# Decay factors of two SSD groups made during the gate products, scans done in place

## The chip, the cores and the metric

The kernel runs on one core of one Trainium2 chip. The metric is the device time of one execution in microseconds (us). The kernel before was timed three times: 1971.74, 1972.97 and 1973.63 us, median 1972.97. One further execution was profiled.

The core has five engines that each follow a queue of instructions in order: TensorE (PE), VectorE (DVE), ScalarE (ACT), GpSimd (POOL) and SyncE (SP, which here only issues transfers). ScalarE and GpSimd issue transfers too, in their place in the queue: a transfer that has to wait for something holds up what stands behind it on its engine.

## The reference

One layer of an encoder on 512 positions of 2048 channels, in float32. Beside an attention branch it has a state space branch (SSD) that runs over the sequence forwards and backwards, 32 heads in 4 groups, in 4 chunks of 128 positions:

```
da   = dt * a                                   # per head and position
a_cs = cumsum(da) within a chunk
lmat = exp(segsum(da))                          # lmat[l, s] = exp(a_cs[l] - a_cs[s]) for s <= l, else 0
y_diag = einsum("bclgn,bcsgn->bcgls", C, B) * lmat  applied to x * dt
y_off  = C . state at the chunk's start . exp(a_cs)
y      = y_fwd + y_bwd + d_skip * x ;  y = rmsnorm(y * silu(z))      # z, g_ssm, g_attn = h @ w_in columns
out    = x + (sigmoid(g_ssm) * (y @ w_ps) + sigmoid(g_attn) * (attn @ w_pa)) @ w_o ;  final rmsnorm
```

The decay factors are the point here: for each head and chunk a 128 x 128 matrix of exponentials of running sums of da, forwards below the diagonal and backwards above it, which multiplies the matrix C.B of that chunk.

## The kernel before, in words

Every matrix product is made of three matmuls on halves: a float32 operand is split into a high part (ScalarE casts it, `wh`, `s_h`, `xw_h`) and a low part (VectorE subtracts it, `wl`, `s_l`, `xw_l`). Weights come in tiles of 128 x 1024; three tiles each of `wh` and `wl` go round (L161-162, L535-536). The stages, in us of the profiled execution:

- up to about 113: the norm, the transposes, then the columns x, B and C of group 0 and dt. `dt_make` (L302-327) makes da for all heads and writes it to the scratch `da_d` in DRAM.
- 113 to 557, **the gates**: three products (z, g_ssm, g_attn: `wz`, `wgs`, `wga`), each as seven Strassen products P1 to P7 for each of two column pairs, 42 products of four chunks of 12 matmuls. A chunk's weights are loaded (X, Y or wraw), added where Strassen wants a sum, cast and subtracted (`wh` L458, `wl` L459). Results go through SiLU or sigmoid (L834) and are stored (`put`, L288) by ScalarE's queue.
- 560 to 1100, **the SSD groups** 0 to 3 (`ssd_group`). Each has a start (B, C and x loaded and transposed), a *state part* (`state_in` makes xw, `state` adds `loc` into the running states S0 and S1 and splits them into s_h and s_l, `offdiag` multiplies them into `off`), and a *decay part* of eight jobs (`da_load`, `seg_make`, `diag`): a job takes 4 heads of one chunk. Between all of these, `gap()` puts matmuls of other products (the next group's x, B and C; q, k and v; the attention's gate) as fill.
- then attention, and the output products to the end.

A job of the decay part: SP loads two broadcast tiles `da0` and `da1` (128 x 512, every partition the same row); VectorE scans each into a `sum` tile, with a mask `scn` that restarts the sum at the diagonal (L1135), adds the two, the second reversed (L1138), ScalarE takes Exp (L1139), and the result E multiplies G, which is made from C.B and dt (L1144-1146). `diag` has TensorE apply G to x (`yb`), and VectorE adds `yo` into `y` (L1159).

The order of TensorE's instructions is that of the program, written by hand. The other engines' order is made by a scheduler, which places each instruction where its own cost model finds it ready, within the priorities that `high_priority` gives and the order that `keep_in_program_order` fixes. Tiles come from pools with a fixed number of buffers for each tag; a tile's next user waits for the last reader. The `st` pool has tiles that serve one after another as x, B, C columns under way (`xbc`), as the angles `ta` and `tb` of the rotary part, as `dt64` and as `z`.

Of the kernel before, what the change touches and what calls it, by code (L numbers as in the profile page):

```python
# [72 lines left out]
def build(tc, a):  # L73
# [40 lines left out]
    xbc_d = [[scratch(f"xbc_d{g}_{i}") for i in range(6)] for g in range(GROUPS)]  # L114
    qkv_d = [scratch(f"qkv_d{i}") for i in range(10)]
# [175 lines left out]
    da_d = dr.tile([64, SEQ], F32, name="da_d")  # L291
# [8 lines left out]
    def dt_make(new):  # L300
# [21 lines left out]
        for i in range(2):  # L322
            r0, cs = 64 * i, slice(i * HS, (i + 1) * HS)
            act.dma_start(da_d[0:NH, cs], da2[r0:r0 + NH])
            act.dma_start(da_d[NH:64, cs], pl[r0 + NH:r0 + 64])
            act.dma_start(dt_d[0:64, cs], dt2[r0:r0 + 64])
            act.dma_start(dt_d[64:128, cs], da2[r0:r0 + 64])

# [258 lines left out]

    def product(name, op, chunk, extra=None, pre=None):

        used.append((used[-1] + 1) % 4)  # L590
        bs = [b(name) for b in SETS[used[-1]]]
        for m in range(4):
            raw = chunk(m)
            h, l = w_split(raw)
            if extra:
                extra(m, raw)
            if pre and m == 2:
                pre()
            for i in range(2):
                for jj in range(2):  # L600
# [4 lines left out]
                    pe.matmul(bs[i], xh, wl, start=False, stop=False)  # L605
                    pe.matmul(bs[i], xl, wh, start=False, stop=(j == 7))  # L606
                    yield 3
        product_done()
        return bs
# [217 lines left out]
    for tag, n, w in (("X", 4, 1024), ("p1", 2, SEQ), ("p5", 2, SEQ), ("u", 2, SEQ), ("pad", 2, SEQ), ("Y", 4, 1024)):  # L827
        for _ in range(n):
            wx.tile([P, w], F32, tag=tag, bufs=n, name=f"{tag}_place")
# [59 lines left out]
    gates[1].hooks = {(0, "P5"): [angles]}  # L889
# [6 lines left out]
    run(xbc_gen(0, 3, None))  # L896
    for p_ in gates:
        for cp in range(2):
            run(p_.pair(cp))
# [7 lines left out]
    scan_f, scan_b = scn[:, :SEQ], scn[:, SEQ:]  # L907
# [9 lines left out]
    sw = open_pool("sw", reuse_waits="tile")  # L917

# [76 lines left out]
    def ssd_group(g):  # L995
# [122 lines left out]
        das = deque()  # L1118

        def da_load(c, q):  # L1120
            h0 = g * HPG + q * 4
            das.append([])
            for dd in range(2):
                da = sw.tile([P, 4, P], F32, tag=f"da{dd}", bufs=2, name=f"da{dd}")
                src = da_d[dd * NH + h0:dd * NH + h0 + 4, c * P:(c + 1) * P]
                tc.keep_in_program_order(nc.sync.dma_start(da, src.unsqueeze(0).broadcast_to([P, 4, P])))
                das[-1].append(da)

        def seg_make(c, q):

            h0 = g * HPG + q * 4
            sums = []
            for da, mask in zip(das.popleft(), (scan_f, scan_b)):
                sums.append(tmp2("sum"))
                dve.tensor_tensor_scan(sums[-1], flat(da), mask, 0.0, ALU.add, ALU.mult)  # L1135
            sf, sb = (t.rearrange("p (h l) -> p h l", h=4) for t in sums)
            E = sw.tile([P, 4, P], F32, tag="E", bufs=2, name="E")
            dve.tensor_add(E, sf, sb[:, :, ::-1])  # L1138
            act.activation(flat(E), flat(E), AF.Exp)  # L1139
# [25 lines left out]
        da_load(0, 0)  # L1165
        for c in range(TT):
            cb_make(c)
            for q in range(2):
                G = seg_make(c, q)
                if (c, q) != (TT - 1, 1):  # L1170
                    da_load(c + q, 1 - q)
# [683 lines left out]
```

## Time and profile before

| | us |
|---|---|
| median of three runs | 1972.97 |
| the profiled execution | 1969.35 |
| its span, from the first to the last instruction | 1967.6 |
| PE busy in the span | 1925.9 |
| DVE busy | 1465.5 |
| ACT busy | 1031.3 |
| POOL busy | 249.3 |

The clock granted to TensorE was 0.999 of full speed. An engine's row in a timeline gives the start, the duration, the line, the operation, what it writes and reads, and in brackets for how long the engine sat idle before it and what ended that. Rows of consecutive matmuls overlap: each lasts 0.39 us, and the next begins 0.23 us after it. In the waits of an engine, a row gives who waited for which instruction, the total in us, how many times, and the longest.

### The profile page before, as it was taken

To read this page: it belongs to the slowest core of one execution; us is meant where nothing else is said; L and a number is where in the kernel's file an instruction comes from. 1 tells how busy PE (TensorE), PEld (TensorE's weight loads), DVE (VectorE), ACT (ScalarE), POOL (GpSimd) and SP (SyncE) were. 2 spreads that over 40 slices of the span, in tenths; PEclk is the share of its full clock that TensorE was granted. 3 is DMA by queue.
4 is the path that set the end of the run, shared out by engine and by line. 5 is a ranking of instruction groups with operands and counts; after the bars stand their busy time and mean duration, and the time that the engine had idled before them with its cause. 6 is when DMAs were issued, how large, how long until landed. Compare 5 with 4: busy or idle time off the path is not lost.

```text
span 1967.6 us, 24492 instructions
## 1 busy us (share of the span) xinstructions
PE 1925.9 (98%) x8834; PEld 1589.7 (81%) x8834; DVE 1465.5 (74%) x2064; ACT 1031.3 (52%) x1531; POOL 249.3 (13%) x317
## 2 busy tenths in 40 slices
PE   7999999999999999999999999999999999999998
PEld 5888888888878888877888888888877777888886
DVE  7886676776759869789786467676776888879467
ACT  6444445444464856757747444444455455444344
POOL 0011001001112030030210211111021111100011
PEclk9999999999999999999999999999999999999999
DMA  6469669668654644665554857887389787847447
GB/s 217 166 203 256 164 166 246 157 179 246 143 174 146 206 123 158 211 196 184 165 166 138 241 173 200 212 221 203 102 221 317 231 274 278 288 160 241 159 90 169
DMA packets 170233, 383.27 MB, mean 195 GB/s; under 512 B 16704, under 2 KB 66944, under 8 KB 169920
## 3 DMA queue, kind: packets, MB, share of 16 engines
q1 hardware_dynamic: 103680, 234.02, 35.7%
q0 software_dynamic: 30912, 103.82, 23.6%
q10 hardware_dynamic: 35520, 43.87, 6.3%
q8 instruction: 69, 1.13, 0.2%
q14 instruction: 52, 0.43, 0.1%
HBM read 329.55 MB, written 98.17 MB: 217 GB/s over the span
## 4 chain that ended last, share of the span: by engine, by line
PE 81%; DVE 9%; DMA 5%; issue 3%; ACT 2%; POOL 0%; SPq 0%; ACTq 0%; DVEq 0%; POOLq 0%
PE P L605 11%; PE P L606 11%; PE P L604 11%; PE xbc L168 4%; PE xbc L169 4%; PE xbc L170 4%; PE za L170 2%; PE za L168 2%; PE za L169 2%; DVE sum L1135 2%; PE qkv L168 2%; PE qkv L170 1%; PE f L1613 1%; PE qkv L169 1%; PE f L1614 1%
## 5 line engine op out<-in xcount | busy, mean ns | idle before, releaser
L458 ACT CAST wh<-X 128x1024 fp32r<-128x1024 f32 x164 | 172.4, 1054 | 199.4 <-PE P L606 158.6
L459 DVE TENSOR_TENSOR wl<-X,wh 128x1024 fp32r<-128x1024 f32 x164 | 199.7, 1222 | 86.4 <-ACT wh L458 85.9
L164 DVE TENSOR_TENSOR wl<-wraw,wh 128x1024 fp32r<-128x1024 f32 (+2 forms) x150 | 175.0, 1168 | 91.4 <-ACT wh L163 85.8
L163 ACT CAST wh<-wraw 128x1024 fp32r<-128x1024 f32 (+2 forms) x150 | 144.8, 967 | 123.0 <-PE xbc L169 34.4
L459 DVE TENSOR_TENSOR wl<-Y,wh 128x1024 fp32r<-128x1024 f32 x88 | 107.5, 1223 | 66.9 <-ACT wh L458 66.7
L458 ACT CAST wh<-Y 128x1024 fp32r<-128x1024 f32 x88 | 92.6, 1054 | 116.1 <-PE P L606 105.7
L168 PE MATMUL xbc<-h_h,wh 128*128 128x512 f32 x384 | 152.7, 398 | 0.0
L170 PE MATMUL xbc<-h_h,wl 128*128 128x512 f32 x384 | 149.8, 390 | 0.0
L169 PE MATMUL xbc<-h_l,wh 128*128 128x512 f32 x384 | 149.6, 390 | 0.0
L604 PE MATMUL P<-wh,h_h 128*128 128x512 f32 x384 | 149.4, 389 | 0.0
L605 PE MATMUL P<-wl,h_h 128*128 128x512 f32 x384 | 149.4, 389 | 0.0
L606 PE MATMUL P<-wh,h_l 128*128 128x512 f32 x384 | 149.4, 389 | 0.0
L458 ACT CAST wh<-wraw 128x1024 fp32r<-128x1024 f32 x68 | 71.7, 1054 | 111.0 <-PE P L606 58.4
L459 DVE TENSOR_TENSOR wl<-wraw,wh 128x1024 fp32r<-128x1024 f32 x68 | 83.0, 1221 | 59.9 <-ACT wh L458 59.9
L605 PE MATMUL P<-wl,S 128*128 128x512 f32 x288 | 112.2, 389 | 1.1 <-DVE wl L459 1.1
L604 PE MATMUL P<-wh,S 128*128 128x512 f32 x288 | 112.0, 389 | 0.0
L606 PE MATMUL P<-wh,S 128*128 128x512 f32 x288 | 112.0, 389 | 0.0
L170 PE MATMUL za<-h_h,wl 128*128 128x512 f32 x256 | 100.2, 391 | 1.8 <-DVE wl L164 1.8
L168 PE MATMUL za<-h_h,wh 128*128 128x512 f32 x256 | 101.5, 397 | 0.0
L169 PE MATMUL za<-h_l,wh 128*128 128x512 f32 x256 | 99.7, 390 | 0.0
L170 PEld LDWEIGHTS xbc<-h_h,wl 128*128 128x128 f32 x384 | 72.1, 188 | 15.5
L1365 ACT ACTIVATE pr<-s,nm 128x512 f32<-128x512 f32 x64 | 44.1, 689 | 76.7 <-DVE nm L1363 76.6
(746 smaller groups left out, 5079.5 us busy)
## 6 DMA issues: line engine op xcount, KB each, us to landing
wraw<-wi SPq DMA_DIRECT2D x102, 512.0 KB, 3.6
T_wps<-wps POOLq DMA_DIRECT2D x32, 512.0 KB, 11.1
da<-da_d SPq DMA_DIRECT2D x64, 256.0 KB, 4.1
T_wpa<-wpa POOLq DMA_DIRECT2D x32, 512.0 KB, 9.4
wraw<-wps SPq DMA_DIRECT2D x24, 512.0 KB, 6.1
wraw<-wo SPq DMA_DIRECT2D x20, 512.0 KB, 3.3
xbc_d<-xbc ACTq DMA_DIRECT2D x24, 256.0 KB, 2.7
wraw<-wun SPq DMA_DIRECT2D x16, 384.0 KB, 5.4
```

Of the source, the lines that this page charges most:

```text
L163: act.copy(h, raw)
L164: dve.tensor_sub(l, raw, h.bitcast(F32))
L168: pe.matmul(out, wh, xh, start=start, stop=False)
L169: pe.matmul(out, wh, xl, start=False, stop=False)
L170: pe.matmul(out, wl, xh, start=False, stop=stop)
L458: i = act.copy(hi_, raw)
L459: dve.tensor_sub(lo_, raw, hi_.bitcast(F32))
L604: pe.matmul(bs[i], xh, wh, start=(j == 0), stop=False)
L605: pe.matmul(bs[i], xh, wl, start=False, stop=False)
L606: pe.matmul(bs[i], xl, wh, start=False, stop=(j == 7))
L1135: dve.tensor_tensor_scan(sums[-1], flat(da), mask, 0.0, ALU.add, ALU.mult)
L1365: act.activation(pr, s, AF.Exp, bias=nm, scale=SCALE, accum_out=sm_)
```

## The change

It has four parts.

1. The decay factors of groups 2 and 3 (16 jobs) are made while the gate products run, and written to new scratch tensors `e_d`. A list of ticks runs one step of a job ahead of a weight chunk: `e_scan(n, 0)`, `e_scan(n, 1)` (with the add), `e_exp(n)` (Exp, the store, the next load). Three tiles e0, e1 and e2 of the `st` pool are used; all transfers are on ScalarE's queue. The mask `scn` is loaded once more, before the gates. `angles()`, the positions' sines and cosines, is called ahead of the gates rather than from a hook within.
2. `da_d` now has the layout [direction, chunk, head, position], so that a job's source is one row of 2 KB for 4 heads.
3. In the SSD groups 0 and 1, the scans work in place on the loaded tiles (`E`, four buffers), and the add writes into the first. In groups 2 and 3 a job loads one finished tile from `e_d`, and there is no scan, no add and no Exp.
4. In the pool of the SSD groups (`sw`), the places for the tags r, E, G, cbf, cbb, yz, yo and xT are taken first, so that the loaded B, C and x tiles lie at other addresses, over the operand sums of the gates.

The core of the diff:

```diff
-    da_d = dr.tile([64, SEQ], F32, name="da_d")
+    da_d = dr.tile([2, TT, NH, P], F32, name="da_d")
...
-            act.dma_start(da_d[0:NH, cs], da2[r0:r0 + NH])
-            act.dma_start(da_d[NH:64, cs], pl[r0 + NH:r0 + 64])
+            for dd, t in enumerate((da2, pl)):
+                act.dma_start(da_d[dd, 2 * i:2 * i + 2].rearrange("c h l -> h c l"), chunked(t)[r0 + dd * NH:r0 + dd * NH + NH])
...
+    def seg_load(queue, ts, dd, g, c, q):
+        src = da_d[dd, c, g * HPG + q * 4:g * HPG + q * 4 + 4].rearrange("h l -> (h l)")
+        tc.keep_in_program_order(queue.dma_start(ts[dd], src.unsqueeze(0).broadcast_to([P, SEQ])))
+
+    def seg_scan(t, dd):
+        return dve.tensor_tensor_scan(t, t, scn[:, dd * SEQ:(dd + 1) * SEQ], 0.0, ALU.add, ALU.mult)
+
+    def seg_add(f, b):
+        return dve.tensor_add(heads4(f), heads4(f), heads4(b)[:, :, ::-1])
...
         for m in range(4):
+            f = ticks.popleft() if ticks else None
+            if f:
+                f()
             raw = chunk(m)
...
-    gates[1].hooks = {(0, "P5"): [angles]}
...
+    angles()
+    scn = wx.tile([P, 2 * SEQ], F32, tag="scn", bufs=1, name="scn")
+    act.dma_start(scn, a["scn"])
+    e_t = [st(f"e{i}") for i in range(3)]
...
+    def e_room(n):
+        return e_t[n % 2], e_t[2]
+
+    def e_load(n, dd):
+        if n < len(e_jobs):
+            seg_load(act, e_room(n), dd, *e_jobs[n])
+
+    def e_scan(n, dd):
+        pin(seg_scan(e_room(n)[dd], dd))
+        if dd:
+            pin(seg_add(*e_room(n)))
+        else:
+            e_load(n + 1, 0)
+
+    def e_exp(n):
+        t = e_room(n)[0]
+        pin(act.activation(t, t, AF.Exp))
+        pin(act.dma_start(e_d[e_jobs[n]], t))
+        e_load(n + 1, 1)
...
+    free = [i for i in range(4, 156) if i // 4 % 7 not in (1, 3)]
+    for n in range(len(e_jobs)):
+        i = n * (len(free) - 3) // (len(e_jobs) - 1)
+        for k, f in enumerate((lambda n=n: e_scan(n, 0), lambda n=n: e_scan(n, 1), lambda n=n: e_exp(n))):
+            ticks[free[i + k]] = f
...
+    for tag, n, shape in (("r", 6, [P, SEQ]), ("E", 4, [P, SEQ]), ("G", 2, [P, 4, P]), ("cbf", 2, [P, P]), ("cbb", 2, [P, P]),
+                          ("yz", 2, [P, SEQ]), ("yo", 1, [P, TT, SEQ]), ("xT", 1, [P, TT, SEQ])):
...
+        def e_fetch(c, q):
+            if (g, c, q) in e_d:
+                es.append([e_tile()])
+                tc.keep_in_program_order(nc.sync.dma_start(es[-1][0], e_d[g, c, q]))
+            else:
+                es.append([e_tile(), e_tile()])
+                for dd in range(2):
+                    seg_load(nc.sync, es[-1], dd, g, c, q)
...
-                dve.tensor_tensor_scan(sums[-1], flat(da), mask, 0.0, ALU.add, ALU.mult)
...
+            if len(ts) == 2:
+                for dd, t in enumerate(ts):
+                    seg_scan(t, dd)
+                seg_add(*ts)
+                act.activation(ts[0], ts[0], AF.Exp)
```

TensorE's and POOL's orders are unchanged. Elsewhere the scheduler moves instructions. In the listings below a row is a line of the kernel, an operation, and its tiles with their numbers; lines of the changed kernel are shifted (L458 has become L472, L1079 L1136, L1135 L338).

ScalarE at the start of the gates, before. X_945 and X_947 are the weights of the first two chunks of the second product (X0' and X1' below), xbc_d0_3 is the store of group 0's last x columns:

```order
L458 CAST wh_1074<-X_951 128x1024
L860 DMA tb_2284<-pos 32x128
L416 ACTIVATE xbc_1014<-xbc_1014 128x512
L288 DMA xbc_d0_3_96<-xbc_1014 128x512
L458 CAST wh_1101<-X_945 128x1024
L458 CAST wh_1120<-X_947 128x1024
```

and in the changed kernel:

```order
L879 DMA tb_1037<-pos 32x128 x4
L472 CAST wh_1135<-X_966 128x1024
L430 ACTIVATE xbc_1029<-xbc_1029 128x512
L289 DMA xbc_d0_3_96<-xbc_1029 128x512
L472 CAST wh_1162<-X_960 128x1024
L335 DMA e0_1077<-da_d_509 128x512
L472 CAST wh_1181<-X_962 128x1024
```

The four loads of the positions have moved ahead of the cast before, and e0's load has come in between the casts of X0' and X1'; e0 takes the place in the `st` pool that xbc_1029 had, and waits for the store from it.

VectorE in group 0's state part, from the second round's decay of S1 to the third round's s_l, before (left out where the dots are: the second round's xw_l, tmp and wl):

```order
L1075 TENSOR_TENSOR S0_4581<-S0_4581,loc_4682 128x512
L164 TENSOR_TENSOR wl_4820<-wraw_4817,wh_4819 128x1024
L1079 TENSOR_TENSOR s_l_4689<-S0_4581,s_h_4688 128x512
L1075 TENSOR_TENSOR S1_4591<-S1_4591,loc_4692 128x512
L1074 TENSOR_TENSOR S0_4581<-S0_4581,dec_4371 128x512
L1079 TENSOR_TENSOR s_l_4699<-S1_4591,s_h_4698 128x512
...
L1079 TENSOR_TENSOR s_l_4792<-S0_4581,s_h_4791 128x512
L1079 TENSOR_TENSOR s_l_4802<-S1_4591,s_h_4801 128x512
```

and in the changed kernel:

```order
L338 SCALAR_TENSOR_TENSOR E_5031<-E_5031,scn_4495 128x512
L1132 TENSOR_TENSOR S0_4733<-S0_4733,loc_4834 128x512
L1132 TENSOR_TENSOR S1_4743<-S1_4743,loc_4844 128x512
L165 TENSOR_TENSOR wl_4972<-wraw_4969,wh_4971 128x1024
L1136 TENSOR_TENSOR s_l_4841<-S0_4733,s_h_4840 128x512
L338 SCALAR_TENSOR_TENSOR E_5032<-E_5032,scn_4495 128x512
L1136 TENSOR_TENSOR s_l_4851<-S1_4743,s_h_4850 128x512
...
L1136 TENSOR_TENSOR s_l_4944<-S0_4733,s_h_4943 128x512
L338 SCALAR_TENSOR_TENSOR E_5055<-E_5055,scn_4495 128x512
L338 SCALAR_TENSOR_TENSOR E_5056<-E_5056,scn_4495 128x512
L338 SCALAR_TENSOR_TENSOR E_5106<-E_5106,scn_4495 128x512
L1136 TENSOR_TENSOR s_l_4954<-S1_4743,s_h_4953 128x512
```

Five scans of group 0's first jobs, and one add where the dots are, now stand ahead of rows of the state part; the decay of S0 stands behind the second s_l.

VectorE in group 1's state part, before:

```order
L1071 COPY S0_5753<-loc_5749 128x512
L1071 COPY S1_5763<-loc_5759 128x512
L1079 TENSOR_TENSOR s_l_5756<-S0_5753,s_h_5755 128x512
L1074 TENSOR_TENSOR S0_5753<-S0_5753,dec_4371 128x512
L1079 TENSOR_TENSOR s_l_5766<-S1_5763,s_h_5765 128x512
```

and in the changed kernel:

```order
L338 SCALAR_TENSOR_TENSOR E_6186<-E_6186,scn_4495 128x512
L338 SCALAR_TENSOR_TENSOR E_6187<-E_6187,scn_4495 128x512
L338 SCALAR_TENSOR_TENSOR E_6210<-E_6210,scn_4495 128x512
L1136 TENSOR_TENSOR s_l_5884<-S0_5881,s_h_5883 128x512
L341 TENSOR_TENSOR E_6186<-E_6186,E_6187 128x512
L1136 TENSOR_TENSOR s_l_5894<-S1_5891,s_h_5893 128x512
```

Three scans and an add of the decay part have moved in between the copies of the first states and their low halves.

More of the change, by code (lines that the diff above doesn't have):

```diff
@@ L114, in build @@
     xbc_d = [[scratch(f"xbc_d{g}_{i}") for i in range(6)] for g in range(GROUPS)]
+    e_d = {(g, c, q): scratch(f"e_d{g}{c}{q}") for g in range(2, GROUPS) for c in range(TT) for q in range(2)}
     qkv_d = [scratch(f"qkv_d{i}") for i in range(10)]
@@ L826, in build @@
     cols = part_ = wx
-    for tag, n, w in (("X", 4, 1024), ("p1", 2, SEQ), ("p5", 2, SEQ), ("u", 2, SEQ), ("pad", 2, SEQ), ("Y", 4, 1024)):
+    for tag, n, w in (("X", 4, 1024), ("p1", 2, SEQ), ("p5", 2, SEQ), ("u", 2, SEQ), ("scn", 1, 1024), ("Y", 4, 1024)):
         for _ in range(n):
@@ L896, in build @@
     run(xbc_gen(0, 3, None))
+    angles()
+    scn = wx.tile([P, 2 * SEQ], F32, tag="scn", bufs=1, name="scn")
+    act.dma_start(scn, a["scn"])
+    e_t = [st(f"e{i}") for i in range(3)]
+    e_jobs = list(e_d)
+    pin = tc.keep_in_program_order
+    def e_room(n):
[15 more added lines that the diff above has]
+    for dd in range(2):
+        e_load(0, dd)
+    ticks.extend([None] * 168)
+    free = [i for i in range(4, 156) if i // 4 % 7 not in (1, 3)]
[3 more added lines that the diff above has]
+            ticks[free[i + k]] = f
     for p_ in gates:
@@ L917, in build @@
     sw = open_pool("sw", reuse_waits="tile")
+    for tag, n, shape in (("r", 6, [P, SEQ]), ("E", 4, [P, SEQ]), ("G", 2, [P, 4, P]), ("cbf", 2, [P, P]), ("cbb", 2, [P, P]),
+                          ("yz", 2, [P, SEQ]), ("yo", 1, [P, TT, SEQ]), ("xT", 1, [P, TT, SEQ])):
+        for _ in range(n):
+            sw.tile(shape, F32R if tag == "r" else F32, tag=tag, bufs=n, name=f"{tag}_place")
     def tmp2(name, n=SEQ):
@@ L1116, in cb_make, with e_tile @@
             cbs[c] = (cbf, cbb)
[L1118 to L1127, printed above, removed]
+        es = deque()
+        def e_tile():
+            return sw.tile([P, SEQ], F32, tag="E", bufs=4, name="E")
+        def e_fetch(c, q):
[4 more added lines that the diff above has]
+                es.append([e_tile(), e_tile()])
+                for dd in range(2):
+                    seg_load(nc.sync, es[-1], dd, g, c, q)
         def seg_make(c, q):
             h0 = g * HPG + q * 4
[L1132 to L1139, printed above, removed]
+            ts = es.popleft()
+            if len(ts) == 2:
[3 more added lines that the diff above has]
+                act.activation(ts[0], ts[0], AF.Exp)
+            E = heads4(ts[0])
             G = sw.tile([P, 4, P], F32, tag="G", bufs=2, name="G")
@@ L1164, in ssd_group @@
         last = None
-        da_load(0, 0)
+        e_fetch(0, 0)
         for c in range(TT):
```

6 lines of the change are left out of this document (4 added, 2 removed).

## The prediction

> **What bounds the kernel now.** I read the page first, then the busy time by stage, then what TensorE waited for, stage by stage. The page:
>
> ```profile
> span 1967.6 us, 24492 instructions
> ...
> PE 1925.9 (98%) x8834; PEld 1589.7 (81%) x8834; DVE 1465.5 (74%) x2064; ACT 1031.3 (52%) x1531; POOL 249.3 (13%) x317
> ```
>
> TensorE is busy 98% of the span and its program order is the same before and after. So the time can only move by TensorE's waits: each one that goes shortens the kernel by its length, each new one lengthens it. Work taken off VectorE is worth nothing in itself. By stage (stretch in us, its length, busy time of PE, PEld, DVE, ACT, POOL, then clock, DMA share, GB/s):
>
> ```profile
> 113.00:557.00 444.00, 442.86 (x1954) 366.47 (x1953) 310.91 (x319) 212.96 (x239) 53.68 (x66) 1.00 0.71 191
> 557.00:617.00 60.00, 57.91 (x271) 47.46 (x270) 40.28 (x54) 32.38 (x50) 16.38 (x12) 1.00 0.46 155
> 617.00:684.00 67.00, 67.00 (x332) 56.51 (x331) 61.54 (x117) 48.01 (x86) 2.97 (x2) 1.00 0.59 185
> 684.00:740.00 56.00, 54.97 (x259) 45.00 (x258) 37.69 (x52) 33.57 (x60) 15.66 (x11) 1.00 0.45 139
> ```
>
> The gates (first row) leave TensorE 1.1 us of wait in 444. Group 0's decay part (third row) has VectorE busy 61.5 of 67.0 us, and yet TensorE misses nothing. So groups 0 and 1 have no wait there that could be won. Groups 2 and 3 have; these are TensorE's waits from 890 to 950 us, and from 1000 to 1060 us (total, times, longest):
>
> ```profile
> PE yb L1156 <- DVE G L1146: 1.8, 2, 1.1
> PE za L170 <- DVE wl L164: 1.0, 1, 1.0
> PE qkv L170 <- DVE wl L164: 0.3, 1, 0.3
> ```
>
> ```profile
> PE yb L1156 <- DVE y L1159: 1.7, 1, 1.7
> ```
>
> All four have VectorE late, among the scans. That is what part 3 of the change can win: 1.8 + 1.0 + 0.3 + 1.7 = 4.8 us, and no more.
>
> **The change part by part.** The pieces of a job, as VectorE and ScalarE run them (count, then min/median/max in ns):
>
> ```profile
> L1135 DVE TENSOR_TENSOR_SCAN sum<-da,scn x64: 1187/1212/2247, 617.0 to 1032.0; 128x512 f32<-128x512 f32 x64
> L1138 DVE TENSOR_TENSOR E<-sum x32: 660/683/693, 625.2 to 1052.3; 128x512 f32<-128x512 f32 x32
> ```
>
> ```profile
> L1139 ACT ACTIVATE E<-E x32: 613/632/636, 627.3 to 1059.3; 128x512 f32<-128x512 f32 x32
> L1139 ACT ACT_TABLE_LOAD  x21: 1283/1283/1283, 626.0 to 1058.0; - x21
> ```
>
> Groups 2 and 3 lose 32 scans and 16 adds: 32 x 1.21 + 16 x 0.68 = 49.7 us of VectorE, some 25 us per decay part of 60. The waits there are at most 1.7 us each, so I take them all as gone: **-4.8 us**. The bounds are 0 (the new loads arrive late) and -4.8.
>
> *Start of the gates: +2.0 us.* The job's first load, e0, stands on ScalarE's queue between the casts of X0' and X1' (first listing in the section on the change), and it reuses the tile whose last reader is the store xbc_d0_3. ScalarE there, and that store's landing time:
>
> ```profile
> 108.56 0.35 ACTq L288 DMA_DIRECT2D xbc_d<-xbc  x1
> 110.04 1.05 ACT L458 CAST wh<-X 128x1024 fp32r<-128x1024 f32 x1 [1.51 <-DMA X<-wz]
> 113.64 1.05 ACT L458 CAST wh<-X 128x1024 fp32r<-128x1024 f32 x1 [2.55 <-DMA X<-wz]
> ```
>
> ```profile
> xbc_d<-xbc ACTq DMA_DIRECT2D x1, 256.0 KB, 9.1
> ```
>
> The store lands at 108.56 + 9.1 = 117.66. ScalarE then issues the load (0.35) and casts X1' (1.05): 119.06. VectorE's low half (1.22) is ready at 120.3. In the old kernel that half ran at 116.83, and TensorE read it at 118.57:
>
> ```profile
> 116.83 1.22 DVE L459 TENSOR_TENSOR wl<-X,wh 128x1024 fp32r<-128x1024 f32 x1
> ```
>
> ```profile
> 118.57 0.39 PE L605 MATMUL P<-wl,S 128*128 128x512 f32 x1
> ```
>
> ```profile
> 98.00:118.00 20.00, 18.86 (x84) 15.28 (x83) 12.48 (x17) 9.49 (x12) 4.66 (x6) 1.00 1.04 313
> ```
>
> That is a wait of 1.7 us. Further casts queued behind the load are X2' and X3', needed 2.72 us apart, so they follow in its shadow. Two things can shift it: the masks' 512 KB and e0's 256 KB come into a stretch that the DMA engines fill already (share 1.04, 313 GB/s), where 768 KB are 2.5 us; and TensorE's 1.1 us wait just before (in which VectorE waits for the positions) may go, since the positions are now asked for together. Bounds 0 to +4.2 (1.7 + 2.5); I take 2.0, close to the 1.7.
>
> *The gates' body: +1.5 us.* Cadence and margin, from ScalarE, then VectorE, then the landing of the gates' stores:
>
> ```profile
> 183.82 1.05 ACT L458 CAST wh<-X 128x1024 fp32r<-128x1024 f32 x1 [0.61 <-PE P L606]
> 186.54 1.05 ACT L458 CAST wh<-X 128x1024 fp32r<-128x1024 f32 x1 [1.67 <-PE P L606]
> ```
>
> ```profile
> 184.91 1.23 DVE L459 TENSOR_TENSOR wl<-X,wh 128x1024 fp32r<-128x1024 f32 x1 [1.50 <-ACT wh L458]
> ```
>
> ```profile
> DMA to landing us min/median/max: 3.6/4.7/9.6
> ```
>
> A chunk takes 186.54 - 183.82 = 2.72 us. Three tiles each of wh and wl exist, so a cast starts as TensorE lets go of the chunk three back and is needed two chunks later: 2 x 2.72 = 5.44 us, of which cast and subtraction take 2.3. The margin is 3.1 us. A job puts two scans and an add (3.1 us) on VectorE over two or three chunks with 1.5 us idle in each; Exp and two table loads (3.2 us) on ScalarE beside 1.67 idle per chunk. Both fit the margin. What may not fit: in five of the sixteen jobs, the reload of a tile stands on ScalarE's queue one cast behind the store from that tile. Counted from the cast ahead of the store (0), the store goes out at 1.05, lands at 5.75 with the median 4.7, and the reload goes out at 6.1, where the next cast was due at 5.44; in two of the five a table load and a SiLU (1.28 + 0.62) stand ahead of that cast, which is then late by 2.6: just inside 3.1. With the longest landing, 9.6, it is late by 7.5 and TensorE waits 4.4. Five of these would be 22 us, none is 0; one landing in three or four that is too slow by about a microsecond gives the 1.5 that I take. The jobs' added traffic (16 x 768 KB) raises the share of 0.71 and pushes that way.
>
> [...]
>
> *Group 0's state part: +4.8 us.* The scans of groups 0 and 1 are now in place, bound no longer to the sum tiles, and the order brings them ahead of the rows that make s_l (second listing above). Before, VectorE made s_l just in time. Two rows of VectorE, then TensorE's two readers:
>
> ```profile
> 603.86 0.69 DVE L1079 TENSOR_TENSOR s_l<-S,s_h 128x512 fp32r<-128x512 f32 x1
> ...
> 613.66 0.69 DVE L1079 TENSOR_TENSOR s_l<-S,s_h 128x512 fp32r<-128x512 f32 x1 [0.58 <-ACT s_h L1078]
> ```
>
> ```profile
> 604.66 0.44 PE L169 MATMUL off<-s_l,c_h 128*128 128x512 f32 x1
> ...
> 615.63 0.39 PE L169 MATMUL off<-s_l,c_h 128*128 128x512 f32 x1
> ```
>
> Second round: two scans stand ahead (2.42) and the decay of S0 moves behind (0.60), so s_l ends at 604.55 + 1.82 = 606.37, 1.7 late. Third round: from one s_l's end to the next it was 614.35 - 604.55 = 9.80. Added: three scans 3.63, the add 0.60, S0's decay 0.60; its wait of 0.58 for ScalarE goes. So 606.37 + 14.05 = 620.42 against 615.63 + 1.7 = 617.33: 3.1 late. Together 4.8. Bounds: 0, if what TensorE reads is late anyway for another reason, and about +10, if each of the five scans takes the longest row (2.25).
>
> [...] The old trace has no scan in a state part, and I stay with the median.
>
> *Group 1's state part: +1.7 us.* The same order, three scans between the copies and s_l (third listing). VectorE's rows, then TensorE's readers:
>
> ```profile
> 714.77 1.27 DVE L1071 COPY S<-loc 128x512 f32<-128x512 f32 x2
> ```
>
> ```profile
> 720.95 0.39 PE L169 MATMUL off<-s_l,c_h 128*128 128x512 f32 x1
> ...
> 732.53 0.39 PE L169 MATMUL off<-s_l,c_h 128*128 128x512 f32 x1
> ```
>
> First round: 716.04 + 3.63 + two rows of 0.60 and one of 0.68 = 721.55, 0.6 late. The 18 rows up to the second round's s_l are 12.7 us at their old steps, so 734.3 against 732.53: 1.7 in all, the third round then just fits. Bounds 0 and +5.
>
> *The rest: 0.* The loads of da move no engine's work but SP's queue; group 0's first tiles, laid elsewhere, still come behind a weight load that waits for a tile of VectorE, as before; dt64's later load has 100 us of gates to hide in, and would cost its landing, some 5 us as for the gates' stores, without.
>
> Sum: -4.8 + 2.0 + 1.5 + 4.8 + 1.7 = +5.2 us. The profiled execution took 1969.35 us around its span of 1967.6; the sum makes 1974.6 of it, and of the median 1972.97, 3.6 above, **1978.2 us**.
>
> **The rivals.** *The early scans cost nothing* (0.30). In the stages with the state parts VectorE idles 60.0 - 40.28 = 19.7 us and 56.0 - 37.69 = 18.3: if the rows it waits for there (s_h, loc) are what really sets s_l, the scans fall into the idle time. Then -4.8 remains, plus up to 3.5 from the gates: 1968.2 to 1971.7, the middle 1969. This is the faster side. Against it: the s_l of 603.86 shows no wait ahead of it.
>
> *The reloads' stores land at the long end* (0.08): the five reloads hold ScalarE, 4 to 22 us more: 1990.
>
> *The decay parts keep their waits* (0.08): the change takes the scans away, and the loads from e_d, one per job on SP's queue behind weights, arrive late instead. 1978.2 + 4.8 = 1983.
>
> [...]
>
> **How the numbers follow.** The forecast has 0.50, with its own range from 1973 to 1985. A measurement of this kernel tells 0.2% (3.9 us) from no change. Of the forecast's half, 0.33 is slower by more than that and 0.17 within; of the first rival, 0.24 faster and 0.06 within; the other three (0.20) are slower. So faster 0.24, same 0.23, slower 0.53. The range goes from the full gain without loss, 1967.5, up to the middle of the long rivals, 1988.
>
> **What would show it.** Right: in the new trace TensorE waits for wl near 119 us, for s_l (L1136) in groups 0 and 1 by some 6 us, and has no G, y or wl wait left in groups 2 and 3. Wrong: s_l is in time with scans ahead of it; or TensorE waits for wl or wh all along the gates; or waits for G remain after 890 us, now behind SP's loads of E.

## The result, and the profile after

The changed kernel takes 2002.44 us (median of four runs, 1998.89 to 2005.67), against 1973.28 for the kernel before on the same chip: ratio 1.015, 95% interval 1.0137 to 1.0164. The prediction had 1978.2, with a range up to 1988: the sign is right, the size is not. The profiled execution took 2005.67 us. One execution of kernel K below took 3115.45 us at a granted clock of 0.656 and is left out of its ratio. From the page of the changed kernel, span and engines:

```profile
span 2003.9 us, 24562 instructions
...
PE 1943.4 (97%) x8834; PEld 1595.0 (80%) x8834; DVE 1465.7 (73%) x2064; ACT 1050.2 (52%) x1545; POOL 248.8 (12%) x317
```

The span grew by 36.3 us, and TensorE, with the same 8834 matmuls, is busy 17.5 us longer. So the loss has two parts: 18.8 us in which TensorE waits, and 17.5 us more of busy time for the same work. The same stages as in the prediction, moved to where they lie now (stretch in us, its length, busy time of PE, PEld, DVE, ACT, POOL, then clock, DMA share, GB/s):

```profile
113.00:585.00 472.00, 455.23 (x1955) 369.37 (x1955) 353.94 (x367) 254.83 (x282) 53.57 (x66) 0.99 0.75 207
585.00:652.00 67.00, 60.14 (x271) 47.85 (x270) 47.42 (x60) 37.02 (x54) 16.90 (x13) 0.99 0.42 142
...
719.00:782.00 63.00, 58.91 (x262) 46.55 (x261) 48.00 (x64) 36.88 (x65) 17.36 (x11) 0.97 0.43 138
```

The gates went from 444 to 472 us. TensorE's idle time in them from 1.1 to 16.8 (472.00 - 455.23), and its busy time from 442.9 to 455.2: 15.7 us of waits and 12.4 us of added busy time. Group 0's state part went from 60 to 67 us (waits from 2.1 to 6.9), group 1's from 56 to 63 (1.0 to 4.1). What TensorE waited for, in the gates, then in the two state parts (total, times, longest):

```profile
PE P L624 <- DVE wl L473: 12.3, 14, 2.1
PE P L623 <- ACT wh L472: 4.4, 3, 2.5
...
PE off L170 <- DVE s_l L1136: 3.8, 4, 2.1
...
PE off L170 <- DVE s_l L1136: 1.9, 4, 0.7
PE off L169 <- ACT s_h L1135: 1.3, 2, 0.7
```

From 922 to 1100 us, groups 2 and 3, TensorE has no wait for G, y or wl any more. Behind the gates' waits stand ScalarE and VectorE, both waiting for transfers of the jobs (100 to 610 us; first ScalarE's waits, then VectorE's):

```profile
ACT L853 <- DMA e_d<-e: 12.2, 2, 6.7
ACT wh L472 <- DMA e<-da_d: 12.0, 2, 6.5
...
ACT wh L472 <- DMA xbc_d<-xbc: 6.3, 1, 6.3
ACT wh L472 <- DMA e_d<-e: 6.0, 1, 6.0
```

```profile
DVE e L338 <- DMA e<-da_d: 6.8, 3, 3.5
```

One of the five tight reloads, on ScalarE:

```profile
173.74 0.63 ACT L938 ACTIVATE e<-e 128x512 f32<-128x512 f32 x1
174.28 1.03 ACT L472 CAST wh<-X 128x1024 fp32r<-128x1024 f32 x1
174.41 0.33 ACTq L939 DMA_DIRECT2D e_d<-e  x1
174.77 0.49 ACTq L335 DMA_DIRECT2D e<-da_d  x1
175.43 1.06 ACT L472 CAST wh<-X 128x1024 fp32r<-128x1024 f32 x1
182.82 0.33 ACTq L335 DMA_DIRECT2D e<-da_d  x1
183.18 1.28 ACT L853 ACT_TABLE_LOAD   x1 [6.69 <-DMA e_d<-e]
184.47 0.63 ACT L853 ACTIVATE p<-p 128x512 f32<-128x512 f32 x1
185.01 1.03 ACT L472 CAST wh<-X 128x1024 fp32r<-128x1024 f32 x1
```

The store of 174.41 lets the reload go at 182.82, 8.4 us later, and everything behind it on ScalarE stands. What TensorE makes of it:

```profile
186.09 0.80 PE L623 MATMUL P<-wh,h_h 128*128 128x512 f32 x1 [2.53 <-ACT wh L472]
187.35 0.80 PE L624 MATMUL P<-wl,h_h 128*128 128x512 f32 x1 [0.47 <-DVE wl L473]
187.94 0.63 PE L625 MATMUL P<-wh,h_l 128*128 128x512 f32 x1
188.37 0.63 PE L623 MATMUL P<-wh,h_h 128*128 128x512 f32 x1
```

It waits 3.0 us in two pieces, and then issues matmuls 0.43 us apart instead of 0.23. The profile's row for that stretch gives the clock as half:

```profile
186.00:192.00 6.00, 5.45 (x12) 3.98 (x13) 4.19 (x4) 4.47 (x6) 0.89 (x1) 0.50 0.70 232
```

To find where time is lost, I lined up the 8834 matmuls of two traces one by one (their order is the same) and took how far each stage grew. All later kernels are read in the same way (us against the kernel before; the stages by the old trace's times; columns named as the experiments below):

| | after | A | F | G | H | I | J | K |
|---|---|---|---|---|---|---|---|---|
| gates, 113 to 557 | +27.7 | +27.4 | +2.9 | +11.5 | +15.3 | +7.8 | +4.8 | +4.2 |
| of it TensorE idle | +15.6 | +15.3 | +1.3 | +6.6 | +8.9 | +4.8 | +2.3 | +1.6 |
| groups 0 and 1, 557 to 880 | +15.0 | +3.2 | +13.6 | +14.7 | +14.8 | +1.7 | +1.8 | +0.3 |
| groups 2 and 3, 880 to 1140 | -7.6 | -7.5 | -7.4 | -7.6 | -7.6 | -6.4 | -4.8 | -3.0 |
| everything else | +1.2 | +2.1 | -1.5 | +1.6 | -1.5 | -0.6 | -0.8 | +0.1 |

Within the gates of the changed kernel the steps are: the start +2.3; the first job, 132 to 137 us of the old trace, +5.2; the five tight reloads (175, 251, 328, 404, 480) +6.1, +2.9, +2.0, +2.7 and +2.2, together 15.9; three others +4.2.

Of the 12.1 us there that are not idle time, 6.6 lie in three stretches at half clock (117.8 to 121.2, 141.6 to 145.0 and 186.0 to 192.8 us of the new trace). Another 4.2 belong to the waits themselves: the matmul ahead of a wait counts its full 0.39 us as busy, where the next would have followed after 0.23, and the one behind a wait holds up its successor by 0.11 more. The other 1.3 are spread.

### The profile page after: what moved, and what is told of

Same layout as the page of the kernel before. It is cut to its first block, busy times and chain, and to the rows that moved or that the text cites. A ratio compares the mean times of both kernels' runs of the same rounds, so it can differ in the third digit from the quotient of the medians.

```text
span 2003.9 us, 24562 instructions
## 1 busy us (share of the span) xinstructions
PE 1943.4 (97%) x8834; PEld 1595.0 (80%) x8834; DVE 1465.7 (73%) x2064; ACT 1050.2 (52%) x1545; POOL 248.8 (12%) x317
## 4 chain that ended last, share of the span: by engine, by line
PE 73%; DVE 10%; DMA 10%; ACT 3%; issue 2%; ACTq 0%; SPq 0%; DVEq 0%
PE P L624 8%; PE P L625 8%; PE P L623 8%; PE xbc L169 4%; PE xbc L170 4%; PE xbc L171 4%; DVE wl L473 3%; PE za L169 3%; PE za L171 3%; PE za L170 3%; PE qkv L169 2%; PE qkv L171 2%; PE qkv L170 2%; DMA e_d<-e 2%; ACT wh L472 2%
## 5 line engine op out<-in xcount | busy, mean ns | idle before, releaser
L472 ACT CAST wh<-X 128x1024 fp32r<-128x1024 f32 x164 | 171.2, 1050 | 176.2 <-PE P L625 84.2
L472 ACT CAST wh<-Y 128x1024 fp32r<-128x1024 f32 x88 | 92.3, 1053 | 107.8 <-PE P L625 97.0
L472 ACT CAST wh<-wraw 128x1024 fp32r<-128x1024 f32 x68 | 71.6, 1054 | 107.3 <-PE P L625 57.4
L624 PEld LDWEIGHTS P<-wl,h_h 128*128 128x128 f32 x384 | 72.7, 189 | 23.3 <-DVE wl L473 8.3
L623 PEld LDWEIGHTS P<-wh,h_h 128*128 128x128 f32 x384 | 72.7, 189 | 21.3 <-ACT wh L472 6.1
## 6 DMA issues: line engine op xcount, KB each, us to landing
T_wps<-wps POOLq DMA_DIRECT2D x32, 512.0 KB, 11.5
```

Of the source, the lines that this page charges most:

```text
L472: i = act.copy(hi_, raw)
```

## The experiments

The theory after the result: in the gates the jobs' transfers hold ScalarE and VectorE in place, and the waits and the slower clock behind them are the loss; in groups 0 and 1 it is the early scans. The rivals: the jobs' own work on VectorE and ScalarE is too much for the gates; or the added traffic makes everything late.

**A. Groups 0 and 1: scans and s_l held in program order.**

```diff
-            dve.tensor_sub(s_l, flat(S[dd]), s_h.bitcast(F32))
+            tc.keep_in_program_order(dve.tensor_sub(s_l, flat(S[dd]), s_h.bitcast(F32)))
...
-                    seg_scan(t, dd)
+                    tc.keep_in_program_order(seg_scan(t, dd))
```

> The changed kernel, with VectorE's low halves of the states (s_l) and the scans of groups 0 and 1 held in the program's order, so that no scan stands ahead of an s_l; nothing else differs. Theory (the early scans delay s_l): the 14 us that TensorE loses between 600 and 780 us go, s_l is waited for less than 1 us in all, about 1989 us. Rival (the in-place tiles and their loads are what is slow there): the waits for s_l stay, about 2002 us.

Measured 1994.26 us (1.0101, 1.0086 to 1.0116), 8.2 under the changed kernel; about 1989 had been expected. What is left of the waits for s_l in the whole span, and the longest new one:

```profile
PE qkv L171 <- DVE wl L165: 1.6, 1, 1.6
...
PE off L170 <- DVE s_l L1136: 0.7, 1, 0.7
```

Both state parts are back at their old length (+0.3 and 0.0), and some 3 us are lost in the decay parts instead. So the early scans were the loss there. The rival that they cost nothing has fallen.

**B. The clock: the old kernel with VectorE held up at seven chunks** by extra copies into wl ahead of the subtraction.

```diff
+            for _ in range(late.get(n_chunk[0], 0)):
+                dve.tensor_copy(l, raw)
+            n_chunk[0] += 1
+    late = {30: 4, 44: 5, 58: 6, 72: 4, 86: 8, 100: 5, 114: 12}
```

> The kernel before, with 4 to 12 further copies on VectorE ahead of the low half of one weight chunk at seven places in the gates, so that TensorE waits there for some 1 to 11 us. Theory (a wait of TensorE over about 2 us is followed by a stretch of matmuls at half speed): matmuls 0.43 us apart for some 4 us after the longer waits, and none after those below 1.5 us, so the time grows by the waits and about 2 us more for each long one. Rival (the slow stretches of the changed kernel come from its transfers): 0.23 us apart after every wait.

Measured 1992.84 us in a single execution, the profiled one. TensorE waited for wl at three of the seven places and, for 1.4 us, at the start of the gates, where the old kernel has 1.1. Its waits in the gates, and the stretches after the two longest:

```profile
PE P L611 <- DVE wl L459: 16.1, 4, 8.0
```

```profile
433.00:439.00 6.00, 5.60 (x13) 4.44 (x14) 0.34 (x1) 0.51 (x1) 0.88 (x1) 0.50 0.73 125
...
347.00:353.00 6.00, 5.67 (x18) 4.55 (x19) 0.48 (x2) 1.05 (x1) 0.89 (x1) 0.72 1.01 220
```

The gates lose 20.4 us, 15.0 of it idle. Behind the wait of 8.0 us the clock is 0.50 for 6 us, behind the one of 5.1 it is 0.72; behind the one of 1.4 it stays at 1.00, with 28 matmuls in 6.0 us. So a long wait costs more than itself, with no job and no added transfer in the kernel.

**C. Reloads further from their stores, first attempt.** Reloads come at least five casts after the store; so that the order stays so, the casts are pinned. In the second kernel A is added, and a later start.

```diff
-            split_into(h, l, raw)
+            cast = split_into(h, l, raw)
+            if ticks and len(ticks) < 168 - 12:
+                tc.keep_in_program_order(cast)
...
+    starts = [4 + n * (152 - 4) // (len(e_jobs) - 1) for n in range(len(e_jobs))]
...
+            tick(i + 2 + 5, lambda n=n: e_load(n + 2, 0))
```

> The changed kernel, with each forward tile of the gates' jobs reloaded at least five chunks after the store from it, the casts of the gates' weights held in order against these loads, and the jobs spaced evenly; the same loads, stores, scans and Exps. Theory (ScalarE stands still behind a reload that waits for its tile's store): the five stalls at 186, 267, 346, 427 and 505 us go, with what the clock lost after them, 16 us, about 1986 us. Rival (the jobs' 12 MB of traffic make the weights late): most of the 25 us stay, above 1996 us.

> Both edits, and the masks and the first job's loads only from the fourth product of the gates on, behind the angles' stores. Theory: the gates lose 0 to 3 us against the kernel before, groups 0 and 1 nothing, groups 2 and 3 win 7: 1966 to 1970 us. Rival (traffic): 1975 us or more.

Measured 2197.2 and 2183.1 us. The edit did something else than meant. Of the first kernel's waits, TensorE's longest in total, and one of ScalarE's:

```profile
PE P L625 <- ACT wh L472: 100.4, 37, 5.7
```

```profile
ACT p L855 <- DVE p L677: 39.8, 12, 6.8
```

My reading: a pinned cast can no longer overtake the SiLU of a product's end, which waits for VectorE and TensorE; so each product's end holds up the next product's casts. (Exp, pinned too, stands 46.0 us for VectorE's add, ten times; no run separates the two.) A later pair of kernels, with tiles as in D, casts and low halves pinned, the jobs' steps at their priority, and (second kernel) the old groups 0 and 1, went the same way: 2184.71 and 2172.21 us.

> The changed kernel with the exchanged tiles of the run swap, its first loads from the twentieth chunk of the gates on, a job every 8.7 chunks, and the jobs' scans, Exps, loads and stores held in the program's order among the casts and low halves of the weights, at the same priority: every load is issued about seven chunks (18 us) ahead of its scan, every tile stored some eight casts ahead of its reload. The same transfers and the same work of VectorE and ScalarE. Theory (a job's transfer that is awaited on ScalarE's or VectorE's queue holds up the weights behind it; the transfers of this stage take up to 10 us): the gates lose less than 6 us against the kernel before, about 1984 us with groups 0 and 1 as in the change. Rival (traffic or engine time of the jobs): 20 us or more in the gates, above 2000 us.

> The run hold with groups 0 and 1 as in the kernel before. Theory: 14 us less than hold, about 1968 us, level with the kernel before or faster. Rival: above 1985 us.

None of the four says anything on the theory. They point to casts that need the freedom to overtake.

**D. The tiles' roles exchanged**, so that no load waits for a store: the two directions' tiles change places, and Exp writes into the other one. The same transfers, and the old ticks. The second kernel starts the jobs behind the 16th chunk, the third adds the old groups 0 and 1.

```diff
-        return e_t[n % 2], e_t[2]
+        return e_t[2], e_t[n % 2]
...
-        else:
-            e_load(n + 1, 0)
-        t = e_room(n)[0]
-        pin(act.activation(t, t, AF.Exp))
+        t, o = e_room(n)
+        pin(act.activation(o, t, AF.Exp))
...
+        e_load(n + 1, 0)
```

> The changed kernel with the roles of the gates' three tiles exchanged: the forward sums always in the third tile, the backward ones in turn in the other two, and Exp writes over the backward tile, which is stored. So the tile that is reloaded next was last read by Exp on ScalarE itself, and the stored tile comes back six to fourteen casts after its store. The same transfers, scans, adds and Exps, no order held. Theory (ScalarE stands still behind a reload that waits for its tile's store): the stalls at 186, 267, 346, 427 and 505 us go, about 16 us, 1986 us. Rival (the traffic, or the jobs' time on VectorE and ScalarE): most of them stay, above 1996 us.

> The run before, with the masks and the first job's loads behind the cast of the sixteenth chunk of the gates instead of at their start, and the jobs spread over the chunks from the twentieth on. Theory (e0's load and the first job, among the angles' work, cost the 8 us up to 141 us): 1978 us, with the gates within 3 us of the kernel before. Rival (the masks or the positions, or the jobs anywhere): 1983 us or more, with stalls moved to the later jobs.

> The run before, with groups 0 and 1 as in the kernel before (separate sum tiles for the scans, four tiles for the loads, the scratch rows of 2 KB kept) and the pool's places as before. Theory (the scans in place, free to go ahead, cost groups 0 and 1 some 14 us; groups 2 and 3 win 7): 1965 to 1969 us, faster than both kernels. Rival (what groups 0 and 1 lose comes from 2 KB rows or from later lateness in the gates): 1975 us or more.

Measured 2012.53 (1.02, 1.0185 to 1.0216), 2021.83 and 2010.77 us: all slower than the changed kernel. ScalarE's waits for the jobs' stores are gone (one of 6.2 us, behind the store of the last x columns, stays), and VectorE's for loads have grown from 6.8 us in three places to

```profile
DVE e L338 <- DMA e<-da_d: 21.5, 9, 5.9
```

The load now goes out behind the Exp, and the next job's first scan comes a chunk later. A transfer that is asked for too late holds VectorE as surely as one that waits for its tile holds ScalarE. My expectation had counted only the second.

**E. The same exchange, jobs spread evenly over all products, one cast and one low half pinned for each job**; loads lead their scans by three chunks or more. Alone, then with the old groups 0 and 1.

```diff
+    starts = [18 + n * (157 - 18) // (len(e_jobs) - 1) for n in range(len(e_jobs))]
...
+        held[168 - i] = (False, True)
+        held[168 - i - 2] = (True, False)
```

> The changed kernel with the exchanged tiles of the run swap, the jobs spread evenly over all products from the eighteenth chunk of the gates on, the first loads and the masks from the fourteenth, and in each job only one cast and one low half held in order against the job's steps. In the resulting order every load stands at least three chunks (8 us) ahead of its scan and every stored tile comes back after seven casts or more; the changed kernel has eight pairs with one chunk or none. The same transfers and the same work. Theory (a job's transfer awaited too early on ScalarE's or VectorE's queue holds up the weights): the gates lose less than 8 us where the change lost 28, about 1982 us. Rival (traffic or engine time of the jobs): 20 us or more in the gates, above 1995 us.

> The run even with groups 0 and 1 as in the kernel before. Theory: 12 us less than even, 1966 to 1973 us, level with the kernel before or faster. Rival: above 1982 us.

Measured 2015.46 and 2002.09 us. The jobs' transfers are hardly awaited any more (VectorE 1.5 us, at one place), but the gates lose 37 us. ScalarE's rows in the first kernel:

```profile
ACT p L587 <- PE P L631: 23.4, 18, 4.8
ACT u L859 <- DVE u L681: 14.4, 6, 6.5
```

Again SiLUs and sums of product ends stand ahead of casts. The pins disturb more than they mend, so the pair can't tell the theories apart. The difference of the two, 13.4 us, points the way A does: by the lined-up matmuls the old groups 0 and 1 are 16.0 us shorter, and groups 2 and 3 win 4.3 less.

**F and G. Work and traffic apart.** In F the jobs' scans, adds, Exps and table loads stay and their transfers are left out (they run on constant tiles, and groups 2 and 3 load rows of da). In G the transfers stay, and the scans, adds and Exps in the gates are left out (a constant tile is stored). Neither computes the layer's decay factors of groups 2 and 3.

```diff
# F
-            seg_load(act, e_room(n), dd, *e_jobs[n])
+            pass
...
-        pin(act.activation(t, t, AF.Exp))
-        pin(act.dma_start(e_d[e_jobs[n]], t))
+        pin(act.activation(t, t, AF.Exp, scale=0.0))
# G
-        pin(seg_scan(e_room(n)[dd], dd))
-        if dd:
-            pin(seg_add(*e_room(n)))
-        else:
+        if not dd:
             e_load(n + 1, 0)
...
-        pin(act.activation(t, t, AF.Exp))
-        pin(act.dma_start(e_d[e_jobs[n]], t))
+        pin(act.dma_start(e_d[e_jobs[n]], e_t[2]))
```

> The changed kernel without the jobs' transfers in the gates: the 32 scans, 16 adds and 16 Exps run on tiles that are filled once (Exp with a scale of 0), nothing is loaded or stored, and groups 2 and 3 load a row of da in place of a finished tile. Theory (transfers awaited): the gates lose 3 us or less and the time is about 1980 us, with groups 0 and 1 as in the change. Rival (the engines' time): the gates keep 15 us or more.

> The changed kernel with the jobs' transfers alone: the 32 loads go to two tiles that nobody reads, the 16 stores come from one constant tile, and there are no scans, adds and Exps in the gates. Theory: no engine waits for a transfer, the gates lose 5 us or less, about 1982 us. Rival (12 MB more in the gates make the weights late): the gates keep 15 us or more, above 1992 us.

Measured 1980.17 (1.0034, 1.0021 to 1.0047) and 1989.45 us (1.0078, 1.0053 to 1.0104). TensorE's waits in F's gates are one place, at the start:

```profile
PE P L624 <- DVE wl L473: 2.4, 1, 2.4
```

From there to the end of the gates F loses nothing (0.0 us). So the work of sixteen jobs, table loads included, fits into the gates. The transfers alone cost 11.5 us, and both together 27.7, about twice the sum of 2.9 and 11.5. Each of F and G also lacks what joins the two: a scan that waits for its load, a store that waits for a late Exp. The places say more than the sums. At the first job G loses 5.6 us, as much as the change with its 5.2, and F 0.0: that loss comes with the transfers. Behind the first job the change loses 20.2 us, G 3.3 and F 0.0, so there neither work nor transfers alone do it, but the waits between them. Nor is G pure traffic: ScalarE stands 17.3 us in it behind the jobs' own transfers, where none had been expected.

F settles the start as well. It has no e0 load, and loses 2.9 us there all the same. VectorE in the old kernel and in F:

```profile
113.43 0.23 DVE L862 CAST ta<-tb 128x128 f32<-128x128 int32 x1 [4.49 <-DMA tb<-pos]
...
114.42 1.22 DVE L459 TENSOR_TENSOR wl<-X,wh 128x1024 fp32r<-128x1024 f32 x1
```

```profile
114.34 0.23 DVE L881 CAST ta<-tb 128x128 f32<-128x128 int32 x1 [4.96 <-DMA tb<-pos]
...
115.86 1.22 DVE L473 TENSOR_TENSOR wl<-X,wh 128x1024 fp32r<-128x1024 f32 x1
```

The positions arrive 0.9 us later, and six rows of the angles stand ahead of X0's low half instead of four. That low half is 1.4 us late in F, and 1.2 in the changed kernel, with e0.

**H. The changed kernel with a third forward tile**, in the room that masks in bfloat16 leave; the ticks are as in the change, so that a reload comes ten casts or more after the store from its tile.

```diff
-    scn = wx.tile([P, 2 * SEQ], F32, tag="scn", bufs=1, name="scn")
-    act.dma_start(scn, a["scn"])
-    e_t = [st(f"e{i}") for i in range(3)]
+    scn = wx.tile([P, 2 * SEQ], mybir.dt.bfloat16, tag="scn", bufs=1, name="scn")
+    pool.dma_start(scn, a["scn"])
+    e_t = [st(f"e{i}") for i in range(3)] + [wx.tile([P, SEQ], F32, tag="em", bufs=1, name="e3")]
...
-        return e_t[n % 2], e_t[2]
+        return e_t[(0, 1, 3)[n % 3]], e_t[2]
```

> The changed kernel with one tile more for the forward sums (three in turn instead of two; the room comes from masks kept in bfloat16, loaded by GpSimd's queue). The jobs' places are the same; a stored tile comes back ten casts or more after its store instead of one. Theory (ScalarE behind reloads that wait for a store): the 16 us at 186, 267, 346, 427 and 505 us go, 1986 us. Rival (the planner's order under more work, or the scans that wait for loads, fill the gap): above 1995 us.

Measured 1993.54 us (1.0101, 1.007 to 1.0132), 8.9 less than the changed kernel; between the two expectations. The gates lose 15.3 instead of 27.7, with one wait for a store left on ScalarE, of 1.7 us. The first job costs 0.7 instead of 5.2; the masks are on another queue here and half as large. But the five places of the tight reloads still lose some 10 us of their 15.9, 6.8 of it at the first, although no reload waits for a store there. VectorE waits for loads that go out about one chunk ahead of their scan, 12.7 us at six places:

```profile
181.85 1.23 DVE L338 TENSOR_TENSOR_SCAN e<-e,scn 128x512 f32<-128x512 f32 x1 [2.81 <-DMA e<-da_d]
```

**I. H with the jobs spread evenly over all products, no cast or low half pinned, and the old groups 0 and 1.**

```diff
+    starts = [8 + n * (157 - 8) // (len(e_jobs) - 1) for n in range(len(e_jobs))]
...
-            ticks[free[i + k]] = f
+            ticks[i + k] = f
```

> The run before with the jobs spread evenly over all products from the eighth chunk, and groups 0 and 1 as in the kernel before: from the second job on each load stands two to twelve chunks ahead of its scan, no reload is near its store, and no cast is held in order. Theory (waits for the jobs' transfers): the gates lose less than 10 us, 1966 to 1975 us. Rival (the jobs' work or traffic): 1985 us or more.

Measured 1972.52 us (0.9995, 0.9981 to 1.0009). The 29 us of the change are gone: 20 in the gates (27.7 to 7.8), where loads now lead their scans by more and no reload stands behind a store, and 13 in groups 0 and 1. The same decay factors are still made in the gates, on the same engines. From 100 to 610 us neither TensorE, ScalarE nor VectorE waits for a store of the jobs any more, and VectorE waits for one load of theirs, 2.3 us. So the loss was in how the transfers stood, as the theory has it; but nothing is gained on the old kernel.

**J and K. I with the positions early** (on GpSimd's queue, into the third tile), the first job's loads behind chunk 14 and its scans from chunk 20; in J, Exp one chunk later besides.

```diff
-            act.dma_start(posi[qd * 32:(qd + 1) * 32].bitcast(I32),
+            pool.dma_start(posi[qd * 32:(qd + 1) * 32].bitcast(I32),
...
+    ticks[14] = lambda: [e_load(0, dd) for dd in range(2)]
+    starts = [20 + n * (157 - 20) // (len(e_jobs) - 1) for n in range(len(e_jobs))]
```

> The evenly spaced jobs with a third forward tile and the old groups 0 and 1, and in addition: the positions on GpSimd's queue before the gates (in the third tile, so that VectorE finds them there), the first job's loads behind chunk 14 and its scans from chunk 20, and Exp one chunk later. Theory: the 2.3 us at the start of the gates came from VectorE's wait for the positions in front of the first chunk's low half, and the 1.5 us near 141 from the first job among the angles' rows; both go, and the late Exps cost nothing: gates lose at most 3 us, groups 2 and 3 win 6, time 1966 to 1970. Rival: the start is lost to the traffic and the order of the queue whatever the positions do, and the time stays at 1972.

> The same without the later Exp. Theory: ScalarE stands on Exp until the add is done (4.0 us near 212), with casts behind it; that is worth about 1 us in three or four places, so 1968 to 1973, 1 to 3 us above the kernel with the later Exp. Rival: no difference, since the wait lies inside the margin of 3.1 us.

Measured 1971.1 (0.9998, 0.9988 to 1.0008) and 1970.05 us (0.9994, 0.9985 to 1.0003): no difference from the kernel before, and none between the two, so the late Exp is covered. The positions are asked for at 45.91 us, and VectorE no longer waits for them; the first matmul on X0's low half, 1.4 us late in F, comes 0.8 us earlier than in the old kernel. But 2.8 us are lost again at 121 to 126 us, now by weights that land late. ScalarE in K:

```profile
123.47 2.00 ACT L472 CAST wh<-X 128x1024 fp32r<-128x1024 f32 x2 [3.18 <-DMA X<-wz]
```

The gates lose 4.2 us in K, and groups 2 and 3 win 3.0 instead of 7.6: with their old code a wait of 2.6 us for wl comes back near 1130 us, where the old kernel had 0.8. No version beat the kernel before.

## Why the prediction was wrong in size

*Waits of groups 2 and 3, -4.8: right.* They are gone, and TensorE's idle time there fell by 5.7 us: one more wait for wl, of 0.8 us at 1130, stood outside the two stretches that the prediction read. The stage is 7.6 us shorter.

*Start of the gates, +2.0: near in size (2.3) by luck, wrong in its reason.* The chain of the prediction does stand in the trace: e0's load goes out at 118.22 (117.66 was worked out), and ScalarE stands 6.3 us for it. But F loses 2.9 us without it. I had written that the positions' wait may go since they are now asked for together; it stayed (4.49 us before, 4.58 in the change, 4.96 in F, 4.25 in G), and more of the angles came ahead of the low half.

*The gates' body, +1.5: the step that failed.* It measured some 25 us, in four parts. TensorE waits for wl or wh all along the gates, which the prediction had named as a sign of being wrong.

First, the landing. I took 4.7 us, the median of the old stores, for the five tight reloads, and one in three or four of them too slow, as if by chance. From store to reload it was 8.4, 7.6, 9.3, 8.0 and 8.6 us: all five near what I had called the longest, 9.6. The landing goes by the place. Of the 46 stores of the old gates twelve took 7.2 to 9.6 us and the other 34 took 2.0 to 6.1, and ten of the twelve stand 1 to 6 us ahead of the five places. There the DMA engines were full before the change came (share 0.99 to 1.02 in the old kernel, 1.03 to 1.04 in the new); the 0.71 that I had read is a mean over the whole stage. The old stretch that became that of the first reload, the same in the new kernel, and the landing of the two old stores at 160.95 and 162.12:

```profile
166.60:175.00 8.40, 8.40 (x38) 6.95 (x37) 6.21 (x8) 4.21 (x5) 0.00 (x0) 1.00 1.01 372
```

```profile
174.40:182.80 8.40, 8.40 (x39) 6.96 (x38) 5.86 (x7) 1.97 (x2) 0.00 (x0) 1.00 1.03 356
```

```profile
DMA to landing us min/median/max: 8.9/9.3/9.6
```

So the rows that price the term were in the old trace. The price for five long landings, 22 us, was near the 15.9 measured, though by another sum: it left out the two parts that follow and put a wait of 4.4 us on each, where the first lost 6.1 and the others 2.0 to 2.9. The rival that held it got a chance of 0.08.

Second, the reloaded tile has a reader of its own: a scan on VectorE one chunk later, with the low halves behind it. I had followed the late reload to the next cast, not to the scan (3.50 us of wait there at 184.71). D shows how much it can cost, and H that it is the greater part at the first of the five places.

Third, what a wait costs beyond its idle time: of the 27.7 us only 15.6 are idle, and 6.6 are matmuls at half clock, a term that the old trace's gates did not have (clock 1.00) and the sum did not contain.

Fourth, the first job, +5.2. It fell among the angles' rows, and G has it without any work of the job; the sum had nothing for it.

*Margins were right, for the work.* Two scans, an add, an Exp and two table loads fit each job's chunks: behind its start F loses 0.0 us.

*Group 0's state part, +4.8: right in its waits.* Idle time grew by 4.8 us (2.1 to 6.9), of which the late s_l and s_h are 4.4, and 2.5 us came on top, about half of it at half clock. VectorE, then TensorE, at the third round that the prediction worked out:

```profile
645.17 0.68 DVE L1136 TENSOR_TENSOR s_l<-S,s_h 128x512 fp32r<-128x512 f32 x1
645.77 3.44 DVE L338 TENSOR_TENSOR_SCAN E<-E,scn 128x512 f32<-128x512 f32 x3
649.13 0.66 DVE L1136 TENSOR_TENSOR s_l<-S,s_h 128x512 fp32r<-128x512 f32 x1
```

```profile
649.85 0.51 PE L170 MATMUL off<-s_l,c_h 128*128 128x512 f32 x1 [2.13 <-DVE s_l L1136]
```

Three scans in 3.44 us: they take the median, not the long row of 2.25. But POOL stands idle beside them, from 640.39 to 650.47. The one of the five early scans that ran beside a POOL instruction was long. VectorE, then POOL:

```profile
628.20 2.31 DVE L338 TENSOR_TENSOR_SCAN E<-E,scn 128x512 f32<-128x512 f32 x1
```

```profile
627.69 1.74 POOL L1145 TENSOR_TENSOR yo<-yo,tmp 128x512 f32<-128x512 f32 x1
```

So it is in both kernels: the six long scans of the old one (1.86 to 2.25 us) and the two of the new one (2.06 and 2.31) are just those beside a POOL instruction of the SSD groups, and every other scan of these groups takes 1.19 to 1.23. Why a scan is longer there was not shown. The bound of +10 was not reached because four of the five scans met no POOL instruction; the prediction had priced it by the longest row alone, not by what stands beside each scan.

*Group 1's state part, +1.7: too small.* Waits grew by 3.1 us, since s_h is late as well as s_l (the waits above; xw_l was late before), and 3.2 us came on top, 1.7 of them at half clock.

*The rivals.* Early scans for nothing: fell, by A. E's loads late in groups 2 and 3: fell, no wait there. Of the 0.20 of the other three, 0.04 is for table loads that cost ScalarE more than their 1.28 us. No run shows such a cost: the SiLU of 184.47 starts 0.01 us after the load of 183.18 has ended (183.18 + 1.28), and F, with all the table loads, loses 0.0 us behind its start.

*What is left open.* How much of the 15.9 us at the five places belongs to the cast behind the reload and how much to the scan: H takes only the first away, but moves later rows too. And why weights land late near 121 us once the positions are early.

## What to carry to other kernels

When a transfer that must wait is put on the queue of an engine that also feeds TensorE, price it by the landing of the transfers at that place in the trace, with the DMA share there and not the stage's mean, and follow both of its ends: what stands behind it on the queue, and who reads what it brings. Spare time on the engines is not the test; here the work alone was free and the waits for its transfers cost the most, and one more tile with loads further ahead of their readers won 20 of 28 us back. Pinning an order to mend one wait cost up to 195 us, probably since other instructions had needed the freedom to overtake.

## What the hardware showed that I had not expected

TensorE's granted clock fell to half in steps here, and the length of a wait alone did not decide it. In the trace of the changed kernel, from 110 to 1900 us, there are five stretches at half clock: four last 3.41 us, the one that begins at 186.02 lasts 6.83, and they begin 7, 13, 136 and 36 steps of 3.41 us apart. Eight matmuls fill such a step at half clock, 0.43 us apart instead of 0.23, which costs some 1.6 us. I compared every step at full clock in this trace with the one after it. The five with the most idle time of TensorE, 1.82 to 2.52 us, were each followed by a step at half clock; the other 513, idle for 1.41 us at most, were not. Of the six steps at half clock one had idle time, 0.53 us, and another followed it; the other five had none, and full clock followed.

So it counted how much of a wait fell within one step. Steps of the changed kernel, to a tenth of a us, around the wait of 1.83 us that ends at 116.86, then around the longer one of 2.36 us that ends at 603.86 (stretch, length, busy time of PE, clock, DMA share, GB/s):

```profile
114.30:117.70 3.40, 1.57 (x8) 1.00 1.05 289
117.80:121.20 3.40, 3.40 (x10) 0.51 1.08 242
...
599.10:602.40 3.30, 2.33 (x12) 1.00 1.00 376
602.50:605.80 3.30, 1.94 (x11) 1.00 0.40 161
605.90:609.20 3.30, 3.30 (x20) 1.00 0.02 5
```

The first wait lies in one step, and the next step runs at half clock. The second is split between two, idle for 1.0 and 1.4 us, and the clock stays at 1.00.
